# Attention value products with 65 columns of weights, and row maxima transposed as fp32r products

## The chip, the cores and the metric

The kernel runs on one core of a Trainium2 chip. Its time is device microseconds (us) of one execution; several executions are taken and their median is given. Where a view says PE, PEld, DVE, ACT, POOL and SP, it means the matrix engine's products, its weight loads, the vector engine, the activation engine, GpSimd and the engine that issues most of the DMAs.

## What is computed

One layer of a hybrid block over 1024 latent and 256 context tokens, width 1024: a modulated RMS norm, one input projection, three groups of heads (a Fourier group, grouped-query attention with 8 query heads and 2 key heads, and a gated delta rule that is scanned in both directions), one output projection and a squared-ReLU MLP. The change lies in the attention:

```python
def _attend(q, k, v):
    ...
    def blk(qi):
        s = jnp.einsum('bqhgd,bkhd->bhgqk', qi, k, preferred_element_type=jnp.float32) * scale
        p = jax.nn.softmax(s, axis=-1).astype(v.dtype)
        return jnp.einsum('bhgqk,bkhd->bqhgd', p, v)
    ...
```

Queries are 1024, keys 1280 (the latent ones and the context), the head width is 64.

## The kernel before, in words

Most products are made in fp32r, a rounded form of float32. To keep precision an operand is split in a high part (the rounded value) and a low part (the rest, rounded), and two or three products of the parts are added in PSUM.

Attention runs in 32 blocks `j` of 256 queries (8 heads of 4 blocks), each in 5 steps `n` of 256 keys, so 160 steps. Around a step the loop at lines 1363 to 1395 issues, in this order: one piece of a side task (`side()`: the delta-rule scan, later the Fourier spectra), `values(n)`, `scores(n + 3)`, and one piece of `maxima(j + 2)`.

- `scores` (966 to 979) makes transposed scores, keys on the rows of the array's output: per 128 keys one product with 128 rows of weights and one with 65 rows, whose 65th row subtracts the row maximum of each query. ACT takes the exponential, and the result is split in `hl[:, :, 0]` and `hl[:, :, 1]`.
- `values` (981 to 989) multiplies V by it. `VH` is V's high part beside 64 columns of ones, 128 columns of weights in all, times 512 moving columns (both parts of p); `VL` is V's low part, 64 columns of weights, times 256 moving columns (the high part of p). A step has two of each. Row 64 of the result is the softmax denominator; `finish` (991 to 1031) adds the two halves, fetches rows 0 to 64 and divides by way of a small DMA to DRAM and back.
- `maxima` (941 to 964) makes the plain scores once more, 6 products per block, DVE reduces each to a maximum per query, and two small products with the identity turn the column `mr[:, q]` (128 queries on partitions, one column of weights) into a row at partition 64: `mm(b[64:65, ...], f32(mr[:, q : q + 1]), C["ident"], True, True)`. This is a plain float32 product; the trace has two records for each.
- The side task's scan (1146 to 1208) makes products of 32 x 32, 32 x 64 and 64 x 32 weights, 16 or more at a time, and its pieces stand between the attention's full-size products: one piece ahead of each `values(n)` while the scan lasts.

From line 782 to 1399 (`pinned = True`) the matrix engine's products keep the order in which the program writes them; the other engines' order, and everything after, is set by a scheduler that plays the program through when it is built. All buffers are cut from a few large tiles (`fbase`, `rbase`, `z1a` ... in the trace; `ba` and `bk` are PSUM banks).

Of the kernel before, what the change touches and what calls it, by code (L numbers as in the profile page):

```python
# [14 lines left out]
ALU = mybir.AluOpType  # L15
AX = mybir.AxisListType

P = 128
# [5 lines left out]
NT = S // P  # L24
NCT = CTX // P
NTA = NT + NCT
HD = 64
CK = 32
NCL = S // CK
NCC = CTX // CK  # L30
NCA = NCL + NCC
EPS = 1e-6
# [25 lines left out]
def const_table():  # L58
    p = np.arange(P)
    hb, i = p // CK, p % CK  # L60
    same = hb[:, None] == hb[None, :]
    parts = {
        "ident": np.eye(P),
        "ones": np.ones((P, P)),
        "j32": i[:, None] == np.arange(CK)[None, :],
        "gt": same & (i[:, None] > i[None, :]),
# [5 lines left out]
        "maskcl": hb[:, None] == np.arange(4)[None, :],  # L72
        "mle": i[:, None] <= np.arange(CK)[None, :],
        "mge": i[:, None] >= np.arange(CK)[None, :],
    }
# [101 lines left out]
def view(b, off, *shape):  # L177
    v = Buf.__new__(Buf)
    v.arena, v.shape, v.at = b.arena, (P,) + shape, b.at + off
    v.n = int(np.prod(shape))  # L180
    return v
# [12 lines left out]
def body(tc, t, out):  # L194
# [3 lines left out]
    with ctx:  # L198
# [14 lines left out]
        V, G, T, Y, SC = nc.vector, nc.gpsimd, nc.tensor, nc.sync, nc.scalar  # L213

        def buf(*shape, top=False, a=None, at=None):
            return Buf(a or Fa, (P,) + shape, top, at)

        def rbuf(*shape, a=None):
            return Buf(a or Ra, (P,) + shape)

        def act(o, i, f=AF.Copy, **k):
            return SC.activation(o, i, f, **k)  # L222

        def f32(ap):
            return ap.bitcast(F32)


        def pe(i):
            return tc.keep_in_program_order(i) if pinned else i
# [4 lines left out]
        def mm(o, l, r, start, stop):  # L234
            pe(T.matmul(o, l, r, start=start, stop=stop))  # L235
# [15 lines left out]
        C = {k: cstb[a >= 256]()[:, a % 256 if a < 256 else a - 256 : b if a < 256 else b - 256] for k, (a, b) in CST.items()}  # L251
# [157 lines left out]
        for k, _ in enumerate(mod_steps(0, slabs, bk[2])):  # L409
            b = trb.next()  # L410
# [128 lines left out]
        kc, vc = buf(NCA, HD, a=Z2), buf(NCA, HD, a=Z2)  # L539
        nqb, nkb = buf(NCL), buf(3, NCA)  # L540
        NQ, NK = nqb(), nkb()
# [37 lines left out]
        def q_norm(hp):  # L579
            th, b = thb(), gb.next()[:, 0 : 2 * NCL]  # L580
            for c in range(NCL):
                for h2 in range(2):
                    h = hp * 2 + h2
                    r = slice(64 * h2, 64 * h2 + 64)
                    pe(T.matmul(b[32 * h : 32 * h + 32, 2 * c : 2 * c + 2], th[r, c * CK : (c + 1) * CK], C["ones"][r, 0:2], start=True, stop=True))
                if c % 8 == 7:
                    yield
            r = slice(64 * hp, 64 * hp + 64)
            V.tensor_copy(NQ[r], b[r].rearrange("p (c z) -> p c z", z=2)[:, :, 0])

        def compact(src, hp, dstb, scale):
            for c in range(0, NCA, 8):
                b = gb.next()
                for q in range(8):
                    s, o = (src[0], (c + q) * CK) if c < NCL else (src[1], (c + q - NCL) * CK)
                    for h2 in range(2):
# [36 lines left out]
        b = gb.next()  # L633
# [9 lines left out]
        b = gb.next()  # L643
# [8 lines left out]
        b = gb.next()  # L652
# [5 lines left out]
        for d in range(2):  # L658
# [3 lines left out]
            for c in range(0, NCA, 16):  # L662
                n = min(16, NCA - c)
                b = gb.next()[:, 0 : n * CK]
# [31 lines left out]
        def grams():  # L696
            for c in list(range(NCL, NCA, 8)) + list(range(0, NCL, 8)):
                b = gb.next()
                bv = b[:, 0 : 8 * CK].rearrange("p (c w) -> p c w", w=CK)
                for q in range(8):  # L700
                    for h in range(4):
                        hp, h2 = h // 2, h % 2
                        r = slice(64 * h2, 64 * h2 + 64)
                        k_ = KQT[r, hp, 0, (c + q) * CK : (c + q + 1) * CK] if c < NCL else KTC[r, hp, (c + q - NCL) * CK : (c + q - NCL + 1) * CK]
                        pe(T.matmul(bv[32 * h : 32 * h + 32, q, :], k_, k_, start=True, stop=True))
                for d in range(2):
                    l_ = lst.next()()
                    V.scalar_tensor_tensor(l_, bv, -1.0, FF_[d][:, c : c + 8, :], op0=ALU.mult, op1=ALU.mult)
                    Y.dma_start(lsc[d][:, c : c + 8], l_)
                yield  # L710
            done.append(1)
# [174 lines left out]


        catA = [rbuf(4, S) for _ in range(2)]
        ab = dict(vlh=rbuf(NTA, 3 * HD), mr=[rbuf(8) for _ in range(2)], kv=buf(NTA, 2, HD), q=[buf(NT, HD) for _ in range(2)], p=[buf(512) for _ in range(2)], st=[buf(8) for _ in range(6)])
        qr, pr, str_, mrr = (Ring(ab[k]) for k in ("q", "p", "st", "mr"))  # L890
        ptr_ = Ring([bk[0], bk[1]])
        ld = [[dram.tile([2, S], F32, name=f"l{w}{q}") for q in range(4)] for w in "ab"]
        catAr = [b() for b in catA]
        VH, VL = ab["vlh"]()[:, :, 0 : 2 * HD], ab["vlh"]()[:, :, 2 * HD :]
        kset = [[view(x, 2 * S, S + CTX)() for x in catA]]
        qT0, qm0 = view(catA[0], 0, S)(), [view(catA[1], z * 256, 256)() for z in range(2)]
        hl0 = [view(catA[0], S, 2, 2, 256)(), view(catA[1], 512, 2, 2, 256)()]
# [1 line left out]
        def one_row(kvh):  # L899
            V.tensor_copy(kset[kvh][1][64:65, :], C["ones"][64:65, 0:1].to_broadcast([1, S + CTX]))  # L900

        one_row(0)
        V.tensor_copy(VH[:, :, HD:], C["ones"][:, 0:HD].unsqueeze(1).to_broadcast([P, NTA, HD]))
        s1r = Ring(A3[0:2])
        pvs = [A3[2], bk[2]]
        KVr = ab["kv"]()
# [17 lines left out]
        def v_split(k2):  # L924
            q = slice(k2 * 2, k2 * 2 + 2)
            act(VH[:, q, 0:HD], KVr[:, q, 1, :])
            G.tensor_tensor(VL[:, q, :], KVr[:, q, 1, :], f32(VH[:, q, 0:HD]), op=ALU.subtract)

        def q_load(h):
            qraw[h], qT[h] = qr.next()(), qTr.next()() if h else qT0  # L930
# [10 lines left out]
        def maxima(j):  # L941
            h, gq = j // 4, j % 4
            KH, cols = kset[h // 4][0], slice(gq * 256, gq * 256 + 256)
            qm, mr = qmr.next()() if j > 1 else qm0[j], mrr.next()()
            mx[j] = qm
            act(qm[0:64], qT[h][0:64, cols])
            for n in range(6):
                q, z = n // 3, n % 3
                if z == 0:
                    st4 = str_.next()()  # L950
                o, w = ((0, 512), (512, 512), (1024, 256))[z]
                b = s1r.next()[:, 0:w]
                mm(b, qT[h][:, (gq * 2 + q) * P : (gq * 2 + q + 1) * P], KH[:, o : o + w], True, True)
                V.tensor_reduce(st4[:, z : z + 1], b, AX.X, ALU.max)  # L954
                if z == 2:
                    V.tensor_reduce(mr[:, q : q + 1], st4[:, 0:3], AX.X, ALU.max)
                if n % 2:
                    yield
            yield
            b = s1r.next()  # L960
            for q in range(2):
                mm(b[64:65, q * P : (q + 1) * P], f32(mr[:, q : q + 1]), C["ident"], True, True)
            act(qm[64:65], b[64:65, 0:256], scale=-1.0)
            yield

# [15 lines left out]
        def values(n):  # L981
            k2, hl, pv = n % 5, pt.pop(n), pvs[n // 5 % 2]
            for kk in range(2):
                kb = k2 * 2 + kk
                if kb == 9:
                    mm(pv[0:64, 0:256], VL[:, kb], hl[:, kk, 0], False, False)
                mm(pv, VH[:, kb], hl[:, kk].rearrange("p a b -> p (a b)"), kb == 0, kb == 9)
                if kb < 9:
                    mm(pv[0:64, 0:256], VL[:, kb], hl[:, kk, 0], False, False)

        def finish(j):
            h, gq = j // 4, j % 4
# [44 lines left out]
        def prologue():  # L1037
            kv_load(0)
            q_load(0)
            yield  # L1040
            for q in range(0, NTA, 4):
                k_T(0, q)
                yield
            for q in range(0, NT, 4):
                q_T(0, q)
                yield
            for j in range(2):
                for _ in maxima(j):
                    yield
                scores(j)  # L1050
                v_split(2 * j)
                yield
                v_split(2 * j + 1)
            v_split(4)
# [308 lines left out]
        for n in range(NPR * 5):  # L1363
            j, k = n // 5, n % 5
            if FIRST <= n < LATE:
                side()
            values(n)
            if n + LA < NPR * 5:
                scores(n + LA)
            if k == 0 and j + 2 < NPR:  # L1370
                mxg = maxima(j + 2)
# [114 lines left out]
        for n4 in range(4):  # L1486
# [9 lines left out]
            for q in range(NT):  # L1496
                b = omr.next()[:, 0:256]
# [219 lines left out]
        for pn, (prods, blocks) in enumerate(PASSES):  # L1717
            for pc in range(NPC):
# [14 lines left out]
                if pn == 3 and pc in (2, 3, 4, 5):  # L1733
                    q = pc - 2
                    gated(y11[q], q, 0, lo_h)
                    gated(m3[q], q, 0, hi_h)
                for n in prods:
                    if n in WSUM:
                        x, y, op = WSUM[n]
                        V.tensor_tensor(W[x], W[x], W[y], op=op)  # L1740
                        w = W[x]
                    else:
                        w = W[WRAW[n]]
# [34 lines left out]
```

## Time and profile before

| | us |
|---|---|
| median of 3 runs | 1497.61 (1496.18 to 1501.48) |
| the profiled execution | 1498.84 |
| its span, first to last instruction | 1496.8 |
| PE busy | 1412.0 (94%) |
| PEld busy | 1128.4 (75%) |
| DVE busy | 1028.0 (69%) |
| ACT busy | 705.0 (47%) |
| POOL busy | 658.3 (44%) |

Some 2 us of the profiled execution lie outside the span. Busy shares of PE count records whose ends are modelled and overlap, so a stretch in which PE shows 100% can still hold slack between the starts of its products; the starts in the timeline are what to read.

### The profile page before, as it was taken

How to read it: one execution, taken by the hardware profiler on the slowest of the kernel's cores; microseconds unless marked ns; L12 is line 12 of the kernel's file. 1: busy time of each engine (PE TensorE's matmuls, PEld its weight loads, DVE VectorE, ACT ScalarE, POOL GpSimd, SP SyncE). 2: the span in 40 equal slices, each digit the busy share in tenths (PEclk: the TensorE clock that was granted, in tenths of full speed). 3: DMA queues.
4: the chain of work that ended last, by engine and by line, in shares of the span. 5: the costliest groups of instructions: out<-in, count | busy, mean ns of one | idle time of the engine just before them, and what ended most of it. 6: DMA issues, size and time to landing. Idle time of an engine off the chain costs nothing.

```text
span 1496.8 us, 29025 instructions
## 1 busy us (share of the span) xinstructions
PE 1412.0 (94%) x11502; PEld 1128.4 (75%) x11502; DVE 1028.0 (69%) x1743; ACT 705.0 (47%) x1239; POOL 658.3 (44%) x698
## 2 busy tenths in 40 slices
PE   4899888989999999999999879999999999999998
PEld 1787766666777777768799756888888888888886
DVE  0876687875777777786823798655556577676884
ACT  2743312323767676676602644555555453443331
POOL 2764653623345456456533875444444100020682
PEclk9899999999999999999999979999999999999999
DMA  9414364451001010032332223544444898776641
GB/s 326 169 57 149 91 176 130 139 131 52 9 9 24 2 38 10 9 111 66 98 106 78 103 64 125 170 155 146 150 150 145 294 395 296 237 233 220 195 168 56
DMA packets 137303, 197.66 MB, mean 132 GB/s; under 512 B 45021, under 2 KB 80463, under 8 KB 136911
## 3 DMA queue, kind: packets, MB, share of 16 engines
q1 hardware_dynamic: 136464, 195.12, 40.4%
q8 instruction: 90, 1.47, 0.4%
q10 hardware_dynamic: 703, 0.69, 0.1%
q14 instruction: 46, 0.38, 0.1%
HBM read 149.84 MB, written 45.94 MB: 131 GB/s over the span
## 4 chain that ended last, share of the span: by engine, by line
PE 46%; DVE 4%; POOL 2%; DMA 1%; issue 1%; ACT 0%; SPq 0%; DVEq 0%; POOLq 0%; ACTq 0%
PE bk L239 8%; PE bk L240 8%; PE bk L238 8%; PE ba L239 7%; PE ba L238 7%; PE ba L240 7%; PE bk L235 1%; DVE z1c L1448 1%; DVE fbase L1534 1%; DVE z1b L1315 0%; PE ba L235 0%; DMA fbase<-x 0%; DMA fbase<-la 0%; POOL rbase L1448 0%; DVE z2b L1448 0%
## 5 line engine op out<-in xcount | busy, mean ns | idle before, releaser
L222 ACT ACTIVATE rbase<-fbase 128x512 fp32r<-128x512 f32 (+3 forms) x255 | 172.1, 686 | 92.3 <-PE bk L239 55.3
L222 ACT ACTIVATE fbase<-bk 128x512 f32<-128x512 f32 (+3 forms) x224 | 124.6, 561 | 159.0 <-PE bk L235 111.8
L235 PE MATMUL bk<-rbase 128*128 128x256 f32 (+1 forms) x960 | 167.7, 310 | 2.2 <-DVE rbase L978 1.3
L235 PEld LDWEIGHTS bk<-rbase 128*128 128x128 f32 x960 | 130.7, 182 | 31.0 <-DVE rbase L978 2.0
L222 ACT ACTIVATE z1c<-fbase 128x512 fp32r<-128x512 f32 (+1 forms) x120 | 76.9, 653 | 140.4 <-DMA fbase<-w_ff 50.1
L222 ACT ACTIVATE fbase<-fbase 128x512 f32<-128x512 f32 (+4 forms) x148 | 95.6, 659 | 95.1 <-POOL fbase L1600 25.9
L1481 POOL TENSOR_TENSOR fbase<-fbase 128x512 f32<-128x512 f32 x64 | 88.6, 1386 | 110.7 <-DVE z1c L1448 93.3
L235 PE MATMUL ba<-rbase 128*128 128x512 f32 (+2 forms) x512 | 131.8, 364 | 5.2 <-DVE rbase L978 3.9
L954 DVE TENSOR_REDUCE fbase<-ba 128x1 f32<-128x512 f32 (+1 forms) x192 | 106.8, 596 | 29.4 <-PE ba L235 27.4
L1682 POOL TENSOR_TENSOR z2c<-z2c,fbase 128x512 f32<-128x512 f32 x16 | 31.8, 2005 | 203.3 <-ACT z2c L222 128.0
L222 ACT ACTIVATE rbase<-z1d 128x1024 fp32r<-128x1024 f32 x61 | 63.0, 1054 | 101.0 <-PE bk L239 87.7
L1448 DVE TENSOR_TENSOR z1c<-fbase,z1c 128x512 fp32r<-128x512 f32 x112 | 95.4, 858 | 19.1 <-ACT z1c L222 16.5
L1448 DVE TENSOR_TENSOR rbase<-z1d,rbase 128x1024 fp32r<-128x1024 f32 x61 | 85.7, 1420 | 31.7 <-ACT rbase L222 31.6
L978 POOL TENSOR_TENSOR rbase<-fbase,rbase 128x512 fp32r<-128x512 f32 x56 | 72.3, 1291 | 78.5 <-ACT rbase L222 67.9
L238 PE MATMUL bk<-rbase 128*128 128x512 f32 x256 | 99.6, 389 | 0.0
L239 PE MATMUL bk<-rbase 128*128 128x512 f32 x256 | 99.6, 389 | 0.0
L240 PE MATMUL bk<-rbase 128*128 128x512 f32 x256 | 99.6, 389 | 0.0
L978 DVE TENSOR_TENSOR rbase<-fbase,rbase 128x512 fp32r<-128x512 f32 x104 | 82.2, 791 | 22.1 <-ACT rbase L222 19.5
L1448 DVE TENSOR_TENSOR rbase<-fbase,rbase 128x1024 fp32r<-128x1024 f32 (+1 forms) x63 | 79.9, 1288 | 23.2 <-ACT rbase L222 23.0
L235 PEld LDWEIGHTS ba<-rbase 128*128 128x128 f32 (+1 forms) x512 | 71.9, 174 | 21.4 <-DVE rbase L978 5.3
L239 PE MATMUL ba<-rbase 128*128 128x512 f32 x192 | 74.7, 389 | 0.0
L240 PE MATMUL ba<-rbase 128*128 128x512 f32 x192 | 74.7, 389 | 0.0
(345 smaller groups left out, 3870.6 us busy)
## 6 DMA issues: line engine op xcount, KB each, us to landing
fbase<-w_ff SPq DMA_DIRECT2D x70, 512.0 KB
u<-fbase SPq DMA_DIRECT2D x112, 256.0 KB
z1d<-w_ff SPq DMA_DIRECT2D x34, 512.0 KB
z1d<-u SPq DMA_DIRECT2D x33, 512.0 KB
fbase<-w_mod SPq DMA_DIRECT2D x32, 512.0 KB
fbase<-u SPq DMA_DIRECT2D x23, 512.0 KB
z2a<-w_mod SPq DMA_DIRECT2D x16, 512.0 KB
fbase<-w_in SPq DMA_DIRECT2D x16, 512.0 KB
```

The source lines that it names most:

```text
L222: return SC.activation(o, i, f, **k)
L235: pe(T.matmul(o, l, r, start=start, stop=stop))
L238: pe(T.matmul(o, lh, rh, start=start, stop=False))
L239: pe(T.matmul(o, lh, rl, start=False, stop=False))
L240: pe(T.matmul(o, ll, rh, start=False, stop=stop))
L954: V.tensor_reduce(st4[:, z : z + 1], b, AX.X, ALU.max)
L978: (G if k2 in GP and not any(a <= n < b for a, b in NGP) else V).tensor_tensor(hl[:, :, 1], p, f32(hl[:, :, 0]), op=ALU.subtract)
L1448: eng.tensor_tensor(lo, i, f32(hi), op=ALU.subtract)
L1481: G.tensor_tensor(w[nm], w[a], w[b], op=op)
L1534: sub = lambda e, o, i, x: e.tensor_tensor(o, i, x, op=ALU.subtract)
L1682: G.tensor_tensor(c, c, G2[cs_.start // 512], op=ALU.mult)
```

## The change

V's two parts get one common shape: `VH` keeps its 64 columns and one column of ones (65 columns instead of 128), `VL` gets a 65th column of zeros (65 instead of 64). They stand in one buffer with 68 columns kept for each. The value products write 65 rows of PSUM. For the maxima, `mr` becomes a tile of zeros with 68 columns per query tile, whose 65th column takes the maxima; an fp32r copy of the identity (`identr`) is made once, and the small transposing products become fp32r products of 65 columns of weights that write rows 0 to 64. DVE gets the copy of the identity, two fills with zeros and two short fills of the 65th columns, and loses the fill with 64 columns of ones.

```diff
+VC_ = 68
...
-        ab = dict(vlh=rbuf(NTA, 3 * HD), mr=[rbuf(8) for _ in range(2)], kv=buf(NTA, 2, HD), q=[buf(NT, HD) for _ in range(2)], p=[buf(512) for _ in range(2)], st=[buf(8) for _ in range(6)])
+        ab = dict(identr=rbuf(P), vlh=rbuf(NTA, 2, VC_), mr=[rbuf(2, VC_) for _ in range(2)], kv=buf(NTA, 2, HD), q=[buf(NT, HD) for _ in range(2)], p=[buf(512) for _ in range(2)], st=[buf(8) for _ in range(6)])
...
-        VH, VL = ab["vlh"]()[:, :, 0 : 2 * HD], ab["vlh"]()[:, :, 2 * HD :]
+        VH, VL = (ab["vlh"]()[:, :, w, 0 : HD + 1] for w in range(2))
+        identr = ab["identr"]()
+        V.tensor_copy(identr, C["ident"])
+        for m_ in ab["mr"]:
+            V.tensor_scalar(m_(None, (P, 2 * VC_)), C["ones"][:, 0:1].to_broadcast([P, 2 * VC_]), 0.0, None, op0=ALU.mult)
...
-        V.tensor_copy(VH[:, :, HD:], C["ones"][:, 0:HD].unsqueeze(1).to_broadcast([P, NTA, HD]))
+        V.tensor_copy(VH[:, :, HD], C["ones"][:, 0:NTA])
+        V.tensor_scalar(VL[:, :, HD], C["ones"][:, 0:NTA], 0.0, None, op0=ALU.mult)
...
-                    V.tensor_reduce(mr[:, q : q + 1], st4[:, 0:3], AX.X, ALU.max)
+                    V.tensor_reduce(mr[:, q, HD : HD + 1], st4[:, 0:3], AX.X, ALU.max)
...
-                mm(b[64:65, q * P : (q + 1) * P], f32(mr[:, q : q + 1]), C["ident"], True, True)
+                mm(b[0 : HD + 1, q * P : (q + 1) * P], mr[:, q, 0 : HD + 1], identr, True, True)
...
                 if kb == 9:
-                    mm(pv[0:64, 0:256], VL[:, kb], hl[:, kk, 0], False, False)
-                mm(pv, VH[:, kb], hl[:, kk].rearrange("p a b -> p (a b)"), kb == 0, kb == 9)
+                    mm(pv[0 : HD + 1, 0:256], VL[:, kb], hl[:, kk, 0], False, False)
+                mm(pv[0 : HD + 1], VH[:, kb], hl[:, kk].rearrange("p a b -> p (a b)"), kb == 0, kb == 9)
                 if kb < 9:
-                    mm(pv[0:64, 0:256], VL[:, kb], hl[:, kk, 0], False, False)
+                    mm(pv[0 : HD + 1, 0:256], VL[:, kb], hl[:, kk, 0], False, False)
```

On the matrix engine, around the transposed maxima and the value products of one block in the middle of attention, the program before has this (a row is: line, operation, out<-in, output rows x moving columns, count; `bk_79` and `bk_80` are the scan's banks, `ba_75` and `bk_78` the value products', `bk_77` the scores'):

```order
L235 MATMUL ba_75<-rbase 128x512
L235 MATMUL ba_75<-rbase 64x256 x2
L235 MATMUL ba_75<-rbase 128x512
L235 MATMUL bk_77<-rbase 128x256 x4
L235 MATMUL ba_73<-fbase,rbase 1x128 x2
L235 MATMUL bk_79<-z1b,fbase 32x64 x4
L235 MATMUL bk_80<-z1b,fbase 32x64 x4
L235 MATMUL bk_79<-z1b,fbase 32x64 x4
L235 MATMUL bk_80<-z1b,fbase 32x64 x4
L235 MATMUL bk_79<-z1b,z2a 32x64 x8
L235 MATMUL bk_78<-rbase 128x512
L235 MATMUL bk_78<-rbase 64x256
```

The changed program has at the same place (its lines are one further):

```order
L236 MATMUL ba_75<-rbase 65x512
L236 MATMUL ba_75<-rbase 65x256 x2
L236 MATMUL ba_75<-rbase 65x512
L236 MATMUL bk_77<-rbase 128x256 x4
L236 MATMUL ba_73<-rbase 65x128 x2
L236 MATMUL bk_79<-z1b,fbase 32x64 x4
L236 MATMUL bk_80<-z1b,fbase 32x64 x4
L236 MATMUL bk_79<-z1b,fbase 32x64 x4
L236 MATMUL bk_80<-z1b,fbase 32x64 x4
L236 MATMUL bk_79<-z1b,z2a 32x64 x8
L236 MATMUL bk_78<-rbase 65x512
L236 MATMUL bk_78<-rbase 65x256
```

Nothing has moved on this engine between lines 782 and 1399; only the shapes are others. After that, in the first products of the MLP, the scheduler's order has moved. Before, around a gate product into `bk_76`:

```order
L239 MATMUL bk_80<-z2b,z1c 128x512
L238 MATMUL bk_79<-z2b,z1c 128x512
L239 MATMUL bk_79<-z2b,z1c 128x512
L235 MATMUL bk_76<-fbase 128x256
L240 MATMUL bk_79<-z2b,z1c 128x512
L238 MATMUL bk_79<-z2b,z1c 128x512
```

And with the change, at the same count of products:

```order
L240 MATMUL bk_80<-z2b,z1c 128x512
L241 MATMUL bk_80<-z2b,z1c 128x512
L239 MATMUL bk_79<-z2b,z1c 128x512
L240 MATMUL bk_79<-z2b,z1c 128x512
L241 MATMUL bk_79<-z2b,z1c 128x512
L239 MATMUL bk_79<-z2b,z1c 128x512
```

The gate products come some ten rows later and products into other banks are woven in differently over about 240 rows; the number of products is the same. On DVE the program's first rows change from

```order
L283 MEMSET fbase 83x128
L271 COPY fbase<-bk_77 128x16
L277 SCALAR_TENSOR_TENSOR fbase<-fbase 128x16
L278 TENSOR_SCALAR fbase<-fbase 128x8
L279 TENSOR_SCALAR fbase<-fbase 128x8
```

to

```order
L284 MEMSET fbase 83x128
L897 CAST rbase<-fbase 128x128
L899 TENSOR_SCALAR rbase<-fbase 128x136
L272 COPY fbase<-bk_77 128x16
L278 SCALAR_TENSOR_TENSOR fbase<-fbase 128x16
```

so the copy of the identity and one fill stand ahead of the first copy out of PSUM. On SP one load of x stands ahead of one load of Fourier tables instead of behind it, one load of w_out goes past four small DMAs, and four stores of the MLP's intermediate are shifted by a few places.

## Rows read from the trace of the kernel before

**Rows 1.** The page's first part: busy us (share of the span) and instructions.
```profile
PE 1412.0 (94%) x11502; PEld 1128.4 (75%) x11502; DVE 1028.0 (69%) x1743; ACT 705.0 (47%) x1239; POOL 658.3 (44%) x698
```

**Rows 2.** Busy us by stage: PE, PEld, DVE, ACT, POOL; clock, DMA share, GB/s.
```profile
360.00:655.00 295.00, 293.05 (x4343) 218.61 (x4330) 220.28 (x540) 203.53 (x419) 142.25 (x184) 1.00 0.07 18
655.00:745.00 90.00, 82.36 (x510) 67.94 (x509) 71.41 (x119) 62.53 (x112) 59.58 (x45) 0.96 0.31 98
...
840.00:920.00 80.00, 62.98 (x240) 45.80 (x239) 72.13 (x73) 39.17 (x68) 60.53 (x42) 0.85 0.16 49
```

**Rows 3.** Whom PE waited for, 360 to 655 us: sum, times, longest; the first.
```profile
PE ba L235 <- DVE rbase L978: 1.2, 2, 0.8
```

**Rows 4.** Timeline of PE, 343.9 to 345.1 us: start, us, shape; behind small products.
```profile
344.05 0.50 PE L238 MATMUL bk<-rbase,z1a 128*128 128x512 f32 x1
344.38 0.39 PE L239 MATMUL bk<-rbase,z1a 128*128 128x512 f32 x1
344.61 0.40 PE L240 MATMUL bk<-rbase,z1a 128*128 128x512 f32 x1
```

**Rows 5.** Line 235, scan's products: duration min/median/max ns, first and last start, shapes.
```profile
L235 PE MATMUL bk<-z1b,z2a x1152: 216/216/241, 371.5 to 648.5; 64*32 64x64 f32 x192
...
L235 PE MATMUL bk<-z1b x640: 217/217/266, 376.2 to 643.9; 32*64 32x64 f32 x160
```

**Rows 6.** Timeline of PE, 555 to 563 us; the shape is the first one's.
```profile
558.75 0.64 PE L235 MATMUL bk<-rbase 128*128 128x256 f32 x4
559.32 0.60 PE L235 MATMUL ba<-fbase,rbase 128*1 128x128 f32 x4
559.85 0.46 PE L235 MATMUL bk<-z1b 32*64 32x64 f32 x16
560.24 1.45 PE L235 MATMUL bk<-rbase 128*128 128x512 f32 x8
561.52 0.64 PE L235 MATMUL ba<-rbase 128*128 128x512 f32 x2
```

**Rows 7.** Timeline of PE, 745 to 775 us: neighbours with 256 moving columns.
```profile
745.51 0.28 PE L239 MATMUL ba<-z1c,z2b 128*128 128x256 f32 x1
745.63 0.28 PE L240 MATMUL ba<-z1c,z2b 128*128 128x256 f32 x1
```

**Rows 8.** Groups on PE, 360 to 655 us, shapes apart: count, busy us, mean ns.
```profile
L235 PE MATMUL ba<-rbase 128*128 128x512 f32 x234 | 92.7, 424 | 1.2 <-DVE rbase L978 1.2
...
L235 PE MATMUL bk<-rbase 128*128 128x512 f32 x123 | 52.7, 447 | 0.0
...
L235 PE MATMUL ba<-fbase,rbase 128*1 128x128 f32 x104 | 15.5, 272 | 0.0
```

**Rows 9.** The same groups over the whole span: transposed maxima, and weight loads.
```profile
L235 PE MATMUL ba<-fbase,rbase 128*1 128x128 f32 x128 | 19.3, 272 | 0.0
...
L235 PEld LDWEIGHTS ba<-rbase 128*128 128x128 f32 x352 | 60.7, 190 | 19.7 <-DVE rbase L978 5.3 <-DVE fbase L954 2.0 <-issue 0.4
...
L235 PEld LDWEIGHTS ba<-rbase 128*64 128x64 f32 x160 | 21.9, 137 | 1.7
```

**Rows 10.** Timeline of PE, 663.2 to 664.5 us: transposed maxima with no scan behind them.
```profile
663.44 0.60 PE L235 MATMUL ba<-fbase,rbase 128*1 128x128 f32 x4
663.97 0.85 PE L235 MATMUL ba<-rbase 128*128 128x512 f32 x3
```

**Rows 11.** Timeline of all engines at the start.
```profile
5.58 0.17 DVE L271 COPY fbase<-bk 128x16 f32<-128x16 f32 x1 [4.61 <-PE bk L270]
...
10.99 1.08 PE L235 MATMUL bk<-z2a,fbase 128*32 128x256 f32 x8 [5.45 <-DMA z2a<-w_mod]
```

**Rows 12.** Timeline of PE, 884 to 912 us: neighbours among the first MLP products.
```profile
895.19 0.63 PE L240 MATMUL bk<-rbase,z1c 128*128 128x512 f32 x1
895.62 0.63 PE L238 MATMUL ba<-z2b,z1c 128*128 128x512 f32 x1
```

More of the change, by code (lines that the diff above doesn't have):

```diff
@@ L926, in v_split @@
             act(VH[:, q, 0:HD], KVr[:, q, 1, :])
-            G.tensor_tensor(VL[:, q, :], KVr[:, q, 1, :], f32(VH[:, q, 0:HD]), op=ALU.subtract)
+            G.tensor_tensor(VL[:, q, 0:HD], KVr[:, q, 1, :], f32(VH[:, q, 0:HD]), op=ALU.subtract)
         def q_load(h):
```

## The prediction

> **What bounds the kernel now.** I read the page's first part, then the stages, then the starts of PE's products. PE is busy 94% of the span [rows 1]. In the attention with the scan beside it, 360 to 655 us, it is busy 293 of 295 us, and its largest wait for another engine comes to 1.2 us in all [rows 2, 3]; DVE has 220 and ACT 204 us of work there, so both have slack. What PE saves in that stage shortens the kernel. From 655 to 745 us (Fourier spectra, the last two heads) PE has 7.6 us without a record, so there I count half of what it saves. From 840 to 920 us DVE is the busy one, 72 of 80 us, PE idles 17 us and its mean granted clock is 0.85 [rows 2]; this stage starts when what lies ahead of it ends, and moves earlier with it.
>
> **How the starts read.** After a run of small products the first 512-column product shows 0.50 us and the next one starts 0.33 us behind it; the one after that starts 0.23 us on, and shows 0.40 us [rows 4]. So the first costs about 0.10 us more: its load of 128 columns of weights stands open, where later ones lie under the product ahead. (By durations 0.50 against 0.39 to 0.40; I use 0.105.) The extra goes with the number of columns: with 32 columns of weights the first product shows 241 instead of 216 ns, with 64 columns 266 instead of 217 [rows 5], that is 25, 49 and 105 ns, near 0.8 ns a column each time.
>
> A second cost is seen at the transposed maxima. Four 256-column score products start at 558.75; such starts lie 0.119 us apart [rows 7], so the next product could start at 559.23, but the transposition starts at 559.32 [rows 6]: about 0.09 us for going over to a one-column product at partition 64. Its four records and the way out take 0.53 us to the scan's products, which is 4 x 0.108 and again 0.09 [rows 6]. I read 0.108 as 128 columns in a plain float32 record, two of which make one product: 0.216 us.
>
> **The change, part by part.**
>
> *VH with 65 columns.* 65 columns at 0.8 ns leave about 0.052 us of open load, 0.053 less than now. It counts where a value product is the first full-size one behind the scan's. The means of 424 and 447 ns over 234 and 123 products, against about 392 undisturbed, hold 14.3 us of such extra [rows 8], 136 products' worth at 0.105; walking through the trace in order I count 126 that are value products. 126 x 0.053 = 6.7 us, all between 360 and 655 us. Bounds: nothing, if a load of 65 columns is as dear as one of 128; 126 x 0.056 = 7.1, if it costs what 64 cost. Everywhere else the load lies under a 256-column product, and is worth nothing.
>
> *VL with 65 columns.* One more column and no other shape: nothing. It stays covered by VH's 512 columns.
>
> *Transposed maxima.* There are 128 records, 32 blocks [rows 9], 26 of them between 360 and 655 us [rows 8]; one lies ahead, five behind. The new product covers rows 0 to 64 like its neighbours, so the way in, 0.09, should go. The way out to the scan stays, since the scan's small products follow (26 blocks, counted over the whole trace). 26 x 0.093 = 2.4 us. In the other six a full-size product follows [rows 10]: the way out goes too, and with it the open load behind it, 0.093 + 0.094 + 0.105 = 0.29 us each; one of them lies in the PE-bound stage and five in the later one at half: 0.3 + 0.7 = 1.0 us.
>
> *The new product's own length* has no row: the trace shows no fp32r product with fewer than 256 moving columns. The ends are 0.060 us, half of the 256-column fp32r product's 0.119 [rows 7], and 0.216, the plain product with the same 128 columns. I take 0.216: it is the only row with this width, and what fp32r gives at 256 columns need not hold at half of them. With it this term is zero; at the other end it is 2 x 0.156 x 29.5 blocks (27 and half of five) = 9.2 us more.
>
> *Fills.* The two new DVE instructions at the start wait, like the product whose result the copy behind them fetches, for the table of constants. DVE sits idle for 4.6 us until 5.58, and the first product that needs its result starts at 10.99, on weights from DRAM [rows 11]: nothing, and at most 0.4 us were that cover gone. The fills before attention replace a longer one while PE is full. SP's swaps cost a DMA's issue each, in places where queue and data are ahead: nothing.
>
> *The order of the first MLP products.* Same products, other weave. I take nothing, within 3 us either way, the size of the single waits there (PE idles 17 us in all [rows 2]).
>
> Sum: 6.7 + 2.4 + 1.0 = 10.1 us. DVE and ACT get as much work in less time, so I take off 0.4: **9.7 us**. Made against the profiled execution, 1498.84 becomes 1489.1; that execution was 1.2 above the median of the runs, so for the median 1497.6 - 9.7 = **1488**.
>
> **Two rules against the rows.** The value products show a load of 128 columns that costs twice one of 64: 105 against 49 ns open, and 190 against 137 ns in records [rows 4, 5, 9]. The Trainium skill, "TensorE: Matmul & The Clock Gate", section "Weight-path perf modes — Fast Weight Load (FWL) and DoubleRow", has a fast load, in theory four times as fast, that is on when there are exactly 128 weights and the type is not FP32. By it, 65 columns would cost more than 128, and the term of 6.7 us would turn into a loss of about 3 (a quarter of 128 columns is 32, so 33 columns more at 0.8 ns, 126 times). The trace speaks against it for this type, since a load of 128 shows no faster pace.
>
> Eight products start between 560.24 and 561.52: two VH, two VL, four scores, 2 x 0.234 + 6 x 0.119 + 0.105 = 1.29 us, which is all of the 1.28 [rows 4, 6, 7]. So going from 128 to 64 columns and back costs nothing now. The Trainium skill, "TensorEngine Tiling (Array Packing)", section "Key Properties", says that a change of tiling mode drains the engine. It agrees with the 0.09 at the maxima; at VH and VL, where the trace shows none, the common shape would by it save 288 drains.
>
> **Rivals.**
>
> - *The narrow fp32r product is fast.* For: at 256 columns it runs at one column a cycle. Against: no row of this width. The term of 9.2 us comes on top: 1479.
> - *A load of 65 columns is not half a load.* If it is rounded up to 96 columns, 3.3 us of the 6.7 are left (1491); if to 128, none (1494.6); if 128 columns had a fast pace that 65 lack, with a loss of 3 us, 1498. For: 65 has no row. Against: 32, 64 and 128 columns lie on one line.
> - *The gain is given back.* The last blocks wait for DVE, and the stage of 840 to 920 us too; if what comes earlier only waits longer there, 1496. For: PE's idle time there. Against: those DVE chains start from what PE delivers, so they move.
> - *Slower, by the new weave of the first MLP products.* PE takes its products in order; one whose halves are not yet split holds up those behind it. When PE idles there its clock falls to its lower level: neighbours start 0.43 us apart instead of 0.23 [rows 4, 12]. It ends over 1502 if this costs 14 us: 5 us more idle, about what the worst wait costs now, and some 45 products at the low clock instead of the high. Against: DVE's work there, which sets the pace, is the same. 1503.
> - *VH and VL do drain today.* 288 x 0.09 = 26 us more: 1462. The eight products above speak against it.
>
> **How the numbers follow.** Forecast 0.50 (1485 to 1491); fast narrow product 0.28; load rounded up 0.07; given back 0.09; slower 0.05; drains 0.01. A measurement of this kernel can tell some 0.3%, 4.5 us, from no change. Faster by more than that (under 1493.1): the forecast, the fast product, the drains and part of the rounded load, 0.81. Slower (over 1502): 0.05. Same: 0.14. For 8 in 10 the range takes the forecast and the fast product with some uncertainty, and the rounded load: 1478 to 1494.5.
>
> **What would show it.** Behind the scan's products the first value product shows about 0.45 us instead of 0.50, and the next starts 0.28 to 0.29 instead of 0.33 us later. The transposition starts 0.12 us after the last score product, and two records (or four) follow, 0.43 us in sum if slow, 0.12 if fast; from there to the scan again 0.09 more. The stretch from 360 us to the end of the scan is some 9 us shorter. I am wrong if the first value product still shows 0.50, if the way in is still 0.2 us long, or if the stretch is shorter and the end is not.

## The result, and the profile after

| | before | after |
|---|---|---|
| median | 1499.14 (6 runs, 1496.18 to 1501.48) | **1479.99** (6 runs, 1474.01 to 1481.81) |
| ratio, 95% interval | | **0.986** (0.9842 to 0.9877) |
| the profiled execution | 1498.84 | 1475.22 |
| its span | 1496.8 | 1473.1 |

The kernel became 1.4% faster: 19 us between the medians, 23.6 between the two profiled executions. The forecast was 9.7 us. The direction and the range were right; the forecast size was about half of what came. The range reached down to 1478 because it took in the rival with a fast narrow product, and the median lies 2 us inside that end.

The page's first part of the changed kernel, against [rows 1] (lines of the changed kernel are one to six further down):

```profile
PE 1391.9 (94%) x11438; PEld 1118.6 (76%) x11438; DVE 1026.7 (70%) x1747; ACT 704.6 (48%) x1239; POOL 657.2 (45%) x698
```

PE has 64 records fewer: each of the 64 maxima products now leaves one record instead of two. Its busy time falls by 20 us, and that of DVE, ACT and POOL by 1.3 us at most.

To see where the time went I cut both spans at the same instructions: the first reduction of the maxima, the scan's last instruction on DVE, attention's last one on DVE, the last store of x1 (ahead of the MLP), and the first load of w_ff2.

| stretch, us | before | after | difference |
|---|---|---|---|
| up to attention | 343.7 | 342.7 | -1.0 |
| attention with the scan | 301.4 | 286.1 | **-15.3** |
| rest of attention, with the spectra | 114.5 | 113.7 | -0.8 |
| output projection | 81.3 | 80.1 | -1.2 |
| first MLP products | 312.5 | 307.1 | **-5.4** |
| from w_ff2 on | 343.4 | 343.4 | 0.0 |

Two stretches hold 20.7 of the 23.7 us. One is where the forecast looked; the other is where it took nothing. The small ones need not come from the change: the kernel before with the other order of the MLP products (an experiment below, which has nothing else of the change) takes 340.7 us up to attention, 114.5 in the rest of it and 80.1 in the output projection, and over all kernels the first of these goes from 340.7 to 343.9.

**In attention.** This is PE's timeline around the transposed maxima, as in [rows 6] (start, us, shape; `128*65` is rows times columns of weights, and the shape is the first one's of a row):

```profile
546.18 0.64 PE L236 MATMUL bk<-rbase 128*128 128x256 f32 x4
546.66 0.28 PE L236 MATMUL ba<-rbase 128*65 128x128 f32 x2
546.87 0.46 PE L236 MATMUL bk<-z1b 32*64 32x64 f32 x16
547.26 1.40 PE L236 MATMUL bk<-rbase 128*65 128x512 f32 x8
...
552.92 0.45 PE L236 MATMUL bk<-rbase 128*65 128x512 f32 x1
```

The maxima start 0.48 us behind the first of four scores, which is 4 x 0.119 and no gap: the way in is gone. Two records and the way out to the scan take 0.21 us, where [rows 6] had 0.53 with four records. The median from start to start of the two products is 0.062 us; from the second to the scan it is 0.153, which is 0.062 and the way out, 0.09, that stays. From the last score to the scan a block took 0.74 us and takes 0.335. The eight products behind the scan start in 1.24 us (547.26 to 548.50) instead of 1.28, and the first of them, where it stands alone, shows 0.45 us instead of 0.50 [rows 4]. Behind the scan the second value product starts 0.28 to 0.29 us after the first, where it was 0.33 to 0.34.

Where no scan follows, the way out is gone too (timeline of PE, against [rows 10]): the next product starts 0.12 us behind the first of the pair.

```profile
662.34 0.28 PE L236 MATMUL ba<-rbase 128*65 128x128 f32 x2
662.46 0.65 PE L236 MATMUL bk<-fbase,z1b 128*128 128x256 f32 x2
```

**In the first MLP products.** Busy time from the last store of x1 to DVE's first sum of finished products (line 1577, 1583 in the changed kernel), and from a later such sum on to w_ff2 (columns as in [rows 2]; the row in the middle is what lies between). Before:

```profile
840.91:919.77 78.86, 61.84 (x233) 44.79 (x232) 71.06 (x72) 38.94 (x67) 59.50 (x39) 0.85 0.16 49
919.77:943.33 23.56, 23.56 (x103) 19.05 (x102) 19.98 (x29) 14.16 (x27) 11.81 (x9) 1.00 0.63 215
943.33:1153.42 210.09, 210.09 (x909) 170.01 (x909) 122.29 (x187) 108.58 (x186) 92.06 (x66) 1.00 0.46 151
```

and with the change:

```profile
822.65:900.23 77.58, 65.97 (x255) 47.77 (x254) 71.18 (x74) 41.44 (x71) 60.26 (x40) 0.85 0.18 53
900.23:922.45 22.22, 21.47 (x93) 17.15 (x92) 17.60 (x27) 13.50 (x25) 10.88 (x8) 1.00 0.61 217
922.45:1129.74 207.29, 207.29 (x897) 167.75 (x896) 124.71 (x187) 107.22 (x184) 91.25 (x66) 1.00 0.47 153
```

In the first stretch DVE is busy 71 us in either, and the stretch is about as long. PE however gets through 255 products instead of 233 in it, in time that it idled away before. 22 products at 0.23 us [rows 4] are 5 us that need not be done later; behind DVE's first sum the counts are 10 and 12 lower, and the time up to w_ff2 is 229.5 us where it was 233.7.

### The profile page after: what moved, and what is told of

It is laid out like the page before. It is cut to its first block, busy times and chain, and to the rows that moved or that the text cites. A ratio compares the mean times of both kernels' runs of the same rounds, so it can differ in the third digit from the quotient of the medians.

```text
span 1473.1 us, 28890 instructions
## 1 busy us (share of the span) xinstructions
PE 1391.9 (94%) x11438; PEld 1118.6 (76%) x11438; DVE 1026.7 (70%) x1747; ACT 704.6 (48%) x1239; POOL 657.2 (45%) x698
## 4 chain that ended last, share of the span: by engine, by line
PE 46%; DVE 5%; POOL 2%; issue 1%; DMA 1%; ACT 0%; DVEq 0%; POOLq 0%; ACTq 0%; SPq 0%
PE bk L240 8%; PE bk L241 8%; PE bk L239 8%; PE ba L239 7%; PE ba L240 7%; PE ba L241 7%; DVE fbase L1540 1%; PE bk L236 1%; DVE z1c L1454 1%; DVE z1b L1321 0%; DVE rbase L984 0%; DMA fbase<-la 0%; POOL rbase L1454 0%; PE ba L236 0%; POOL z2c L1714 0%
## 5 line engine op out<-in xcount | busy, mean ns | idle before, releaser
L236 PE MATMUL bk<-rbase 128*128 128x256 f32 (+1 forms) x960 | 164.5, 307 | 2.1 <-DVE rbase L984 1.1
L236 PEld LDWEIGHTS bk<-rbase 128*128 128x128 f32 (+1 forms) x960 | 127.0, 173 | 30.4 <-DVE rbase L984 1.9
L236 PE MATMUL ba<-rbase 128*65 128x512 f32 (+4 forms) x576 | 137.7, 341 | 6.3 <-DVE rbase L984 4.6
L236 PEld LDWEIGHTS ba<-rbase 128*65 128x65 f32 (+1 forms) x576 | 75.7, 154 | 23.9 <-DVE rbase L984 5.7
```

## Experiments

The theory at this point had four parts: (a) 65 columns of VH leave less of a load open, (b) the way in to the maxima is gone, (c) a narrow fp32r product is as fast as a wide one, (d) the other weave of the first MLP products lets PE work while DVE sets the pace. The rivals: that one edit carries the whole of attention's gain; that the zero column ended a drain between VH and VL; and that the MLP's gain is chance. All stretches below are cut as above.

| run | median, ratio (95%) | attention with the scan | first MLP products |
|---|---|---|---|
| before | 1499.14 | 301.4 | 312.5 |
| the change | 1479.99, 0.986 (0.9842 to 0.9877) | 286.1 | 307.1 |
| VH with 128 columns | 1487.12, 0.9935 (0.9914 to 0.9956) | 291.5 | 311.0 |
| value products only | 1484.90, 0.9922 (0.9901 to 0.9944) | 294.9 | 308.1 |
| maxima plain, 65 columns | 1487.23, 0.9941 (0.9921 to 0.9961) | 292.8 | 311.3 |
| VL with 64 columns | 1477.80, 0.9872 (0.985 to 0.9895) | 286.5 | 307.2 |
| the change, old weave | 1481.82, 0.9893 (0.9873 to 0.9913) | 286.0 | 311.8 |
| before, new weave | 1491.20, 0.9968 (0.9952 to 0.9983) | 301.5 | 308.1 |
| VH with 97 columns | 1481.13 (one run) | 288.9 | 307.2 |
| gate products later | 1479.11, 0.9876 (0.9857 to 0.9895) | 286.0 | 310.2 |
| the change again | 1475.84, 0.986 (0.9846 to 0.9875) | 286.0 | 308.0 |

Each ratio is to runs of the kernel before on the same chip; the medians come from several chips and are not to be compared with each other. The two stretches are from one profiled execution each.

**VH with 128 columns again** (the rest as changed; the columns behind the ones are other numbers that nothing reads).

```diff
-        VH, VL = (ab["vlh"]()[:, :, w, 0 : HD + 1] for w in range(2))
+        VHL = ab["vlh"](None, (P, NTA, 2 * VC_))
+        VH, VL = VHL[:, :, 0 : 2 * HD], VHL[:, :, VC_ : VC_ + HD + 1]
...
-                mm(pv[0 : HD + 1], VH[:, kb], hl[:, kk].rearrange("p a b -> p (a b)"), kb == 0, kb == 9)
+                mm(pv, VH[:, kb], hl[:, kk].rearrange("p a b -> p (a b)"), kb == 0, kb == 9)
```

> The changed kernel, but VH's weights are 128 columns again (65 wanted ones and 63 neighbours whose output rows are never read). Theory (an open load costs 0.8 ns a column): the first value product behind the scan shows 0.50 us again and the next starts 0.33 to 0.34 us later instead of 0.28 to 0.29; 360 us to the end of the scan gets 6 to 7 us longer than with the change, the transposed maxima stay at 0.06 us a product. In all 6 to 7 us over the changed kernel from this, and up to 5 more where the order of the first MLP products (nearly that of before here) matters. Rival (the column count is worth nothing, all of the gain is the maxima): that stage as with the change, within 1 us.

Attention with the scan came out 5.4 us longer than with the change, a little under what was expected, and the distance behind the scan is back at 0.327 to 0.342 us. The row of its groups (340 to 640 us) shows the old mean duration of [rows 8] again:

```profile
L236 PE MATMUL bk<-rbase 128*128 128x512 f32 x121 | 52.0, 448 | 0.0
```

against, with 65 columns,

```profile
L236 PE MATMUL bk<-rbase 128*65 128x512 f32 x124 | 49.7, 419 | 0.0
```

So (a) is real and has about the forecast size. The maxima stay at 0.062 us, so their speed does not hang on VH's shape. This kernel got an order of the MLP products that is nearer to the old one than to the new, and its stretch there is long (311.0).

**Value products only** (65 columns for VH and VL, maxima as before; the zero tiles and the copy of the identity are left out too).

```diff
...
-                mm(b[0 : HD + 1, q * P : (q + 1) * P], mr[:, q, 0 : HD + 1], identr, True, True)
+                mm(b[64:65, q * P : (q + 1) * P], f32(mr[:, q : q + 1]), C["ident"], True, True)
```

> The value products of the change (65 columns in both), the transposed maxima as before. Here the order of the first MLP products is exactly that of the change. Theory: 6 to 7 us less than before up to the end of the scan (first value product 0.45, next start 0.28 to 0.29), maxima still 0.74 us from the last score product to the scan's next; and, if the order of the first MLP products is worth the 5 us by which that stage shrank, 5 us less there: 11 to 12 us under before. Rival (that stage shrank by chance or through earlier arrival): 6 to 7 us under before in all.

6.5 us less than before in attention, next start 0.28 to 0.288 us behind the scan's first; the maxima read as before, 0.209 + 3 x 0.108 + 0.203. With the new weave, 4.4 us come off in the MLP. The sum, 10.9 us, is what the medians show (1495.79 for the kernel before on that chip, against 1484.90).

**Maxima plain, 65 columns**: the same shape, but not fp32r.

```diff
-                mm(b[0 : HD + 1, q * P : (q + 1) * P], mr[:, q, 0 : HD + 1], identr, True, True)
+                mm(b[0 : HD + 1, q * P : (q + 1) * P], f32(mr[:, q, 0 : HD + 1]), C["ident"], True, True)
```

> The changed kernel, but the transposition is a plain float32 product of the same 65 columns (four records again). Theory (the way in belongs to the one-column product at partition 64, and the rate to the type): the way in stays gone (0.12 us after the last score product), the records lie 0.108 apart, so 0.31 us more per block: 8 to 10 us over the changed kernel by the end of the attention, and up to 5 more where the order of the first MLP products (nearly that of before here) matters. Rival (the way in belongs to the plain type): 0.09 us more per block, 11 to 13 us by the end of the attention.

PE's timeline of one block in the kernel with values only:

```profile
415.80 0.64 PE L236 MATMUL bk<-rbase 128*128 128x256 f32 x4
416.36 0.60 PE L236 MATMUL ba<-fbase,rbase 128*1 128x128 f32 x4
416.89 0.46 PE L236 MATMUL bk<-z1b 32*64 32x64 f32 x16
```

and in this one:

```profile
414.94 0.64 PE L236 MATMUL bk<-rbase 128*128 128x256 f32 x4
415.42 0.60 PE L236 MATMUL ba<-fbase,rbase 128*65 128x128 f32 x4
415.95 0.46 PE L236 MATMUL bk<-z1b 32*64 32x64 f32 x16
```

The way in is gone, 0.48 instead of 0.56 us from the scores' start, though the product is plain float32: it belonged to the shape of one column at partition 64, not to the type. The 0.53 us to the scan are as before, where the change has 0.21: that part is the type's. Attention with the scan is 2.1 us shorter than with values only (b), and 6.7 longer than with the change (c). Up to the end of attention it is 8.3 longer, as expected, but 1.6 of that lies behind the scan, where the granted clock differs too (last section).

**VL with 64 columns**, no zeros in use.

```diff
-                    mm(pv[0 : HD + 1, 0:256], VL[:, kb], hl[:, kk, 0], False, False)
+                    mm(pv[0:64, 0:256], VL[:, kb, 0:HD], hl[:, kk, 0], False, False)
```

> The changed kernel, but VL with 64 columns, without the column of zeros, into rows 0 to 63. Theory (65 and 64 columns of fp32r are one array shape): the same as the changed kernel within 1 us; VH to VL 0.23 us apart where no small product stands ahead. Rival (65 beside 64 columns changes the tiling and drains): 0.09 us for each of 288 changes from VH to VL, up to 26 us over the changed kernel.

286.5 against 286.1 us: the zero column is worth nothing, and going between 65 and 64 columns costs nothing.

**VH with 97 columns** (as with 128 columns, but `VHL[:, :, 0:97]` and `pv[0:97]`).

> The changed kernel, but VH's weights are 97 columns (65 wanted ones and 32 neighbours). Theory (0.8 ns a column): the product behind the scan shows about 0.475 us, the next one starts 0.31 us later, and 360 us to the end of the scan is about half way between the change and the run with 128 columns, 2 to 3.5 us over the change. Rival (loads are rounded up to whole groups of 32 columns): as with 128 columns, 5 to 6 us over the change.

The next product starts 0.306 to 0.315 us behind the scan's first, and attention is 2.8 us longer than with the change, half of the 5.4 that 128 columns cost. The mean duration lies half-way too:

```profile
L236 PE MATMUL bk<-rbase 128*97 128x512 f32 x120 | 49.7, 432 | 0.0
```

419, 432, 448 ns for 65, 97, 128 columns; the median distance to the next start behind the scan is 0.285, 0.309 and 0.337 us. The open load grows nearly evenly with the columns, by 0.75 to 0.9 ns each.

**The weave of the MLP products.** Two kernels cross it with the rest. NOUT is the attention step behind which the first load of w_out is written (and, five steps on, two gate products). Moving it by one step was enough to tip the scheduler: the changed kernel with 152 got exactly the old order of the first MLP products, and the kernel before with 150 exactly the new one.

```diff
-NOUT = 151
+NOUT = 152
```

> The changed kernel with NOUT 152 instead of 151 (the first w_out products start one step later), which brings the order of the first MLP products back to exactly that of before, with all of the change kept. Theory (that order is worth the 4 us by which the stage from the last store of x1 to the first load of w_ff2 shrank): that stage is 4 us longer than with the change, some 312.5 us as before, and the whole 3 to 5 us over the changed kernel. Rival (the stage shrank for another reason): 308 us in that stage, and the whole within 1 us of the changed kernel.

The mirror image, in the kernel before:

```diff
-NOUT = 151
+NOUT = 150
```

> The kernel before with NOUT 150, which gives it exactly the order of the first MLP products that the change has, and nothing else of the change. Theory: 308 us instead of 312.5 in that stage, 3 to 5 us under before in all, up to the end of the scan as before. Rival: no difference from before over 1 us.

The changed kernel with the old order, the stretch from the last store of x1 on:

```profile
825.49:903.61 78.12, 62.21 (x233) 45.32 (x232) 71.05 (x72) 38.96 (x67) 59.50 (x39) 0.83 0.16 49
```

The kernel before with the new order:

```profile
836.68:915.26 78.58, 64.54 (x255) 47.24 (x254) 71.18 (x74) 41.44 (x71) 60.25 (x40) 0.87 0.17 53
```

The counts of 233 and 255 go with the order, not with the shapes, and so does the length of the whole stretch: 311.8 with the old order and 308.1 with the new. The new order is worth 4.7 us in the one kernel and 4.4 in the other, and by the ratios 4.9 and 4.8 us of the whole time, as expected. All other runs fall in line: those with exactly the new order show 307.1 to 308.1, the two with an order nearer to the old one 311.0 and 311.3. Most of it lies behind DVE's first sum: from there to w_ff2 the six runs with exactly the new order take 229.5 us, and the two with exactly the old one 233.6 and 233.7. (d) is shown; it is no chance of a run, but it is a chance of the build.

**Gate products later**, an attempt to get more of the same: four small gate products, behind which MLP products wait in PE's order, written after the next group of them.

```diff
-        for g in range(4):
-            gate_bc(g2b[g // 2]()[:, g % 2 * 256 : g % 2 * 256 + 256], 1, g, 5120 + g * 256, bk[0])
         for nm in ORDER[2:]:
             for j in range(2):
                 w1_prep(j, nm)
             for j in range(2):
                 ff1(j, nm)
+        for g in range(4):
+            gate_bc(g2b[g // 2]()[:, g % 2 * 256 : g % 2 * 256 + 256], 1, g, 5120 + g * 256, bk[0])
```

> The changed kernel with the four gate products of the MLP (plain float32, each waits until DVE has fetched the one before) written behind the first pair's products instead of among them. If the waits around them are what the new order of the first MLP products saves, the stage from the last store of x1 to the first load of w_ff2 goes from 307 to 305 us or less and the kernel 1 to 3 us under the changed one; if the order saves elsewhere, it stays within 1 us of the changed kernel, or loses some.

It missed: the stretch is 310.2 us against 308.0 of the change run beside it. PE has nearly as much done by DVE's first sum (230.0 us are left, against 229.5), but that sum comes 80.2 us after the last store of x1 instead of 78.5. So the waits around these four products are not what the new order saves; which of the moved products does it stays open. The same run beside it, the change once more:

> The changed kernel once more, on the chip of the run beside it, for the comparison: 1474 to 1482 us, the stage from the last store of x1 to the first load of w_ff2 at 307 us.

It repeats 286.0 us in attention and the ratio, 0.986; with 308.0 its first MLP products show what one order varies by from run to run. No version was clearly faster than the change.

## Why the prediction was right or wrong

*What bounds the kernel.* Right: attention with the scan is where PE's own starts set the length, and 15.3 us went there. DVE and ACT had the slack that was read: they are as busy as before, in 15 us less, and PE's waits for DVE in that stretch came to 2.3 us against 1.8.

*VH with 65 columns, 6.7 us.* Right in mechanism and nearly in size. Undone alone it gives 5.4 us, done alone 6.5; from the starts, 124 first value products behind the scan (the prediction counted 126) times some 0.05 us are 6.2. The rival that a load of 65 columns is rounded up fell, since 65 and 97 columns lie on the line of 32, 64 and 128.

*The way in, 2.4 us.* Right: 2.1 us measured between the kernel with values only and the one with plain products of 65 columns. Its cause was put right as well: the shape, not the type.

*Full exits, 1.0 us.* The way out is gone there: from the first of the maxima to the full-size product behind them 0.12 us, which is two products and nothing else, where it was 0.53. How much of it reached the end was not measured apart; the rest of attention is only 0.8 us shorter, with a spread between runs that is larger (below).

*The new product's own length: the step that failed.* The prediction took 0.216 us ("it is the only row with this width"), and the term as zero. The product takes 0.062 us. The other end, 0.060, had been written down, and its 9.2 us stood as a rival with a chance of 0.28. Measured in attention with the scan it is 6.7 us (plain against fp32r). The prediction counted 27 blocks as bound by PE; in this stretch lie 26, 24 of them with the scan behind, and their distances from the last score to what follows the maxima add up to 17.1 us plain and 9.1 with fp32r, 8.0 us apart. What takes the other 1.3 us is not settled: PE's waits for other engines come to 2.3 us in either trace. The wrong judgement was which row is nearest: the plain product shares the width, but it makes two records for each product, while the 256-column neighbours share the type, and it is the type that decides. That the rival's time, 1479, lies within 1 us of the median is partly luck: it added 9.2 us for this, of which 6.7 came in attention, and nothing for the order of the MLP products, which gave another 4.5.

*The order of the first MLP products: the second step that failed.* It was taken as nothing, within 3 us; it is a gain of 4.4 to 4.7. The prediction saw that DVE sets the pace there and concluded that DVE's work, being the same, keeps the stretch as long. That is so. But PE's idle 17 us [rows 2] are room for products that would otherwise come after, when PE is the bound: the gain appears one stretch later. The rival that ended slower looked at the same weave and only at waits that it could add.

*Given back.* It fell: the stretch behind, from 840 us on, moved earlier with what lies ahead of it, as forecast.

*The two rules.* The fast load of the Trainium skill, "TensorE: Matmul & The Clock Gate", section "Weight-path perf modes — Fast Weight Load (FWL) and DoubleRow", is on for exactly 128 weights of a type that is not FP32. (Its table gives the factor of four for fp8, and no gain for FP32; the prediction left that out.) These runs disagree with its being on here: 97 columns cost less than 128 and 65 less than 97. The Trainium skill, "TensorEngine Tiling (Array Packing)", section "Key Properties", says that a change of tiling mode drains the engine. What the runs show at the maxima is in line with it (0.09 us with one column at partition 64, none with 65 columns at partition 0, in either type); between 65 and 64 columns they show no such cost. In which mode a product ran, no trace tells.

*The sum.* One after the other, values only (6.5), way in (2.1) and type (6.7) make up attention's 15.3 us by construction; the starts alone would give 6.3, 2.3 and 8.0. With 4.5 for the weave that is 19.8 us, against 19.1 between the medians. The profiled execution's 23.6 are some 4 more: 3.0 in the three small stretches of the first table, and 0.9 in the first MLP products.

## What to carry to other kernels

When a cost has no row, choose the bound by what the two rows share with the new operation in kind, not by the one number that they share: here the type, with the count of records as its sign, and not the width. A small shape that stands between others costs more than its own length: look at the starts on either side of it, and give it its neighbours' shape if zeros can fill the rest. And where another engine sets the pace, count how many of the bound engine's products get done meanwhile: an order that brings in more of them pays in the next stretch.

## What the runs showed of the hardware that was not expected

An fp32r product with 128 moving columns takes 0.062 us from start to start (the two of a block), half of the 0.119 of 256 columns, while the plain one takes 0.216 in its two records, with one column of weights as with 65.

The rest of attention (scan's end to attention's end) is 113.7 us in the profile of the change, 113.9 in its repetition and 117.7 with the gates later, though every engine has the same instructions in the same order there. PE's granted clock differs. Busy time by stretch in the kernel with the gates later:

```profile
645.00:665.00 20.00, 16.45 (x87) 13.38 (x86) 15.55 (x22) 9.62 (x19) 19.76 (x16) 0.83 0.34 106
655.00:675.00 20.00, 17.50 (x94) 15.03 (x95) 13.54 (x23) 9.49 (x18) 16.68 (x13) 0.83 0.26 83
```

and in the change run beside it:

```profile
645.00:665.00 20.00, 17.16 (x108) 14.35 (x107) 16.84 (x26) 13.79 (x27) 19.42 (x16) 1.00 0.32 106
655.00:675.00 20.00, 17.60 (x116) 15.15 (x115) 14.19 (x25) 11.59 (x21) 15.61 (x12) 1.00 0.29 93
```

A mean of 0.83 says that PE spent part of those 20 us at its lower level, 1.2 instead of 2.4 GHz. From 640 to 680 us it waits for DVE, ACT and POOL in either run, up to 2 us at once; only in the slower one 0.6 us of it are for a POOL line that had itself waited 3.4 us for a load (1.7 in the other). Over all profiles the clock behind the scan's end goes with the time: where no 20-us piece of the first 40 us is under 1.00 (the change, its repetition, values only, before with the new weave) the rest of attention takes 113.7 to 114.5 us; with one at 0.91 it takes 115.4 to 116.8 (four changed kernels; the kernel before shows 114.5 at 0.91); with one at 0.83 it takes 117.5 and 117.7. So 2 to 4 us of a single execution go with this. But the clock is not all of it. The same two products of the maxima, first in the kernel with the gates later (the scan's last instruction starts at 627.6 us):

```profile
654.49 0.98 PE L236 MATMUL ba<-rbase 128*128 128x512 f32 x2 [0.67 <-DVE fbase L960]
```

and in the change run beside it (628.1 us):

```profile
653.44 0.98 PE L236 MATMUL ba<-rbase 128*128 128x512 f32 x2
```

Counted from the scan's end, PE is 1.5 us behind in the slower one by then, through waits, while its granted clock was still 1.00 (645 to 656.9 us; PE was busy 9.9 of these 11.9 us). The clock shows 0.50 from 657 to 664 us; the other 2.3 of the 3.8 us come after the first two products. Whether this makes the spread from 1474 to 1482 us among runs of the change was not shown. The clock of whole executions does not decide it: the runs of the change with 1475.22 and 1481.81 us both have 0.972, and one with 0.926 took 1480.88. What sets off the waits and the lower clock in one execution and not in the next stays open.
